# Where a LayerNorm's residual update runs in a two-layer fp32 decoder: GpSimd or VectorE

## The chip, the cores and the metric

The kernel runs on one core of one Trainium2 chip. The metric is the device time of one execution in microseconds; it is given as the median of the executions shown, with the lowest and the highest.

## What is computed

A decoder trunk of two layers over 256 tokens of width 1024, all in fp32. Each layer is a mixer (sliding-window attention, a state-space layer and a pooling branch, gated and merged), a cross-attention into 256 memory tokens, and a feed-forward part, a dense SwiGLU in layer 0 and eight experts, two per token, in layer 1. Behind each of the six parts stands the same step, on the residual stream x:

```python
def layer_norm(x, g, b):
    mu = jnp.mean(xf, axis=-1, keepdims=True)
    var = jnp.mean(jnp.square(xf - mu), axis=-1, keepdims=True)
    y = (xf - mu) * lax.rsqrt(var + LN_EPS)
    return (y * g + b).astype(x.dtype)
...
    for i in range(DEPTH):
        h = hybrid_mixer(x, ...)
        x = layer_norm(DN_ALPHA * x + h, ln1_g[i], ln1_b[i])
        c = memory_cross_attention(x, mem, ...)
        x = layer_norm(DN_ALPHA * x + c, ln2_g[i], ln2_b[i])
        f = swiglu(x, ...) if i % 2 == 0 else moe_swiglu(x, ...)
        x = layer_norm(DN_ALPHA * x + f, ln3_g[i], ln3_b[i])
```

## The kernel before

**Weights.** TensorE multiplies fp32 numbers in three passes: each number is cut into a high part that the fast fp32 format holds and a low part, the rest, and the product is high x high, low x high and high x low (`mm3`, L279 to L282). The activations are cut once. The weights arrive as chunks of 1 MB, and each half of a chunk is cut when it is first asked for (`parts`): ScalarE copies the 128x1024 half into `whi` (L217), VectorE subtracts that from the raw half into `wlo` (L220). There are three `whi` and three `wlo` buffers and three raw chunks (more in the expert stage); so ScalarE and VectorE cut at most three halves ahead of TensorE, and a half's buffer comes free when its last matmul is done. Half a chunk is eight blocks of 128x128, and so 24 matmuls in the products of 128x256.

**Order of the work.** Every engine takes its own instructions in a fixed order, which a scheduler lays down when the program is built: it simulates the engines, and of the instructions that could go next takes the one of higher priority. An instruction's priority comes from its place in the program; `tc.high_priority()` lifts a whole block, and an offset shifts it. `tc.issue_after(i)` keeps an instruction behind instruction i in that order. A `Line` object (L229) does this for its calls, so that the instructions made through one `Line` are taken in the order of the calls. The profile shows everything made through a `Line` under one line, L237 (or under that of a helper, as L220).

**The LayerNorms.** `layer_norm_in` (L309 to L383) serves five of the six. Four are of kind "xt", and the text calls them by number: **N1** behind the mixer of layer 0 (some 248 to 275 us into the span), **N2** behind its cross-attention (366 to 392), **N3** behind its SwiGLU (588 to 615), **N4** behind the mixer of layer 1 (835 to 862). The fifth, of kind "moe" (from 940), and the last one, inside the expert stage, are not touched. In a LayerNorm of kind "xt", for both halves m of the tokens:

- VectorE adds ALPHA * x to the part's result out of PSUM into `lny` (two buffers `ys`), takes mean and variance (`bst`, `bmv`) and adds EPS (`bve`); GpSimd raises that to the power -0.5 (`brs`, one column); VectorE makes the shift -mean * `brs` (`bnb`, one column, function `shift`).
- ScalarE normalizes `lny` in place, two halves of 512 columns for each m; TensorE transposes it into PSUM (`pt`).
- In four steps q, ScalarE applies gain and shift to the transposed tile, into `lnx` (128x512, two buffers), and VectorE cuts `lnx`: a cast into `xhi` and a subtraction into `xlo`. The text calls these two a pair. The next matmuls of the program take `xhi` and `xlo`, pair by pair.
- Last, x itself is brought up to date, which the next LayerNorm reads, some 80 us later or more: x = lny * g + b in the natural layout, for m = 0 and 1, on rows of 1024. These four instructions run on GpSimd, whose line `gp` holds the two powers and then these. The gains `g` and `b` were loaded by two DMAs at the start.

```python
            for m in range(2):
                gp(GP.tensor_mul, x[:, m, :], ys[m], g)
                gp(GP.tensor_add, x[:, m, :], x[:, m, :], b)
```

While a LayerNorm runs, TensorE is given other work: N1 to N3 stand beside matmuls of the memory's keys (`keys`, operands `m_hi` and `m_lo`, result copied by ScalarE to `xkt`), and so does N4. The high priority of the LayerNorm puts its VectorE work ahead of the `wlo` of the weights; `guard` (L271 to L274) keeps two of the `wlo` behind the last `bnb`.

What follows behind each: N1 the queries of the cross-attention (L280 to L282); N2 the SwiGLU, with VectorE preparing the state-space layer of layer 1 (`bgh`, `tmps`) and GpSimd clearing its tables; N3 the mixer of layer 1, for which GpSimd clears `up`, `sa`, `sb` (L758 to L760) and works out 16 table instructions first (L827 to L834, in `ssm_quad`); N4 the queries again. GpSimd's queue has besides these one early DMA of x (L1021); the weights come over SP's queue.

Of the kernel before, what the change touches and what calls it, by code (L numbers as in the profile page):

```python
# [39 lines left out]
ALPHA = (2.0 * L) ** 0.25  # L40
EPS = 1e-5
NFIFO = 3
NFX = 11
MAGIC = 12582912.0
TWO_PI = 2.0 * math.pi
SIN_SCALE = 6.2831850

# columns of the per-layer parameter block
PC = {}
# [7 lines left out]

# columns of the constant block: for both layers, for the layers' attention, for the routing
CC = {}
# [136 lines left out]
def tile_trunk(ctx, tc, x_in, xt_in, memt_in, w_in, par_in, ln_in, lnt_in, wr_in, br_in, cst_in, out):  # L196
    nc = tc.nc

    V, A, T, GP = nc.vector, nc.scalar, nc.tensor, nc.gpsimd
# [27 lines left out]

    # calls whose instructions an engine takes in the order of the calls
    class Line:  # L229
# [27 lines left out]

    # the two parts of a chunk, each half of it split when it is first asked for
    def parts(raw):
# [24 lines left out]
    x = xp.tile([P, 2, D], F32, name="x")  # L284
# [6 lines left out]

    # the first loads, in the order of their use
    xt = [xp.tile([P, KD, S], F32R, tag=n, name=n) for n in ("xhi", "xlo")]
# [12 lines left out]

    # x <- LayerNorm(ALPHA * x + f); kind "xt" also gives the transposed result in two parts, kind "moe" the natural
    # one in two parts with the router's logits
    def layer_norm_in(l, i, f, end, kind, lp, r):  # L309
        g = lp.tile([P, D], F32, name="lng", bufs=1)  # L310
        b = lp.tile([P, D], F32, name="lnb", bufs=1)
# [8 lines left out]
        ys, pts = [], []  # L320
        dv, ac, te, gp = Line(), Line(), Line(end), Line()
# [51 lines left out]
        if kind == "xt":  # L373
            for m in range(2):
                gp(GP.tensor_mul, x[:, m, :], ys[m], g)
                gp(GP.tensor_add, x[:, m, :], x[:, m, :], b)
        else:
            dv(V.tensor_add, x[:, 1, :], x[:, 1, :], b)
            for m in (1, 0):
                ac(hi_of, xhi[:, m], x[:, m])  # L380
# [13 lines left out]

    # out^T blocks: stationary weights, moving activations
    def ws_gemm(nob, kt, act, sink, first=0, w=None):
# [20 lines left out]

    # natural outputs: stationary activations, moving weights; n columns of up to 512 in `accs`
    def xs_step(accs, act, w, c0, k, nw, first, last):
# [11 lines left out]

    # the last chunk, one accumulator after the other
    def xs_end(accs, act, w, k0, kn, nw, start):
# [30 lines left out]

    # exp of a small tile by range reduction and a polynomial
    def exact_exp(dst, src, t):
# [16 lines left out]

    # (sine of half an angle, cosine of that, the angle's remainder in [-pi, pi])
    def half_angle(sn, cs, rr, th, t):
# [16 lines left out]

    # in steps, for other work to go between them
    def ssm_params(sp, l, mp, par, par2, tmps, b8, b4, b2):
# [27 lines left out]
        r = t("s_r")  # L532
        rr, sn, cs = t("s_rr"), t("s_sn"), t("s_cs")
        for i, _ in enumerate(zip_longest(exact_exp(r, er, t), half_angle(sn, cs, rr, th, t))):
            if i % 7 == 6:
                yield
        # powers 4 to 1 of abar
        apr, api = t4(), t4()
# [5 lines left out]
        yield  # L544
        # f = (abar - 1) / a
        inv, num = t("s_inv"), t("s_num")
        # f abar^3, f abar^2, f abar, f
        fbr, fbi = t4(), t4()
# [33 lines left out]
        yield  # L582
        # four steps at a time: decay r^4, angle 4*rr (in turns, as a short head and a tail)
        r4 = mp.tile(sh, F32, name="r4")
# [12 lines left out]

        # products of one compact matrix with four scalars each, spread into its two diagonal blocks
        def spread(dst, mr, mi, sr, si, ts, neg):
# [17 lines left out]

        # output matrices (C, -C_im), and those times powers of abar
        cx = b4([P, 2, NT, 2, 16], F32, "cx")
        GP.memset(cx, 0.0)  # L620
        for h in range(2):
            o = slice(64 * h, 64 * h + 64)
# [3 lines left out]
        GP.memset(wx, 0.0)  # L626
        # input matrices, by the step of the four, transposed to [(step, channel), state]
        bt = [mp.tile([P, NT, P], F32, name=f"bt{c}") for c in range(2)]
# [22 lines left out]
        yield  # L651
        # the four steps among themselves: blocks (from step i, to step 3 - o) = C abar^(3-o-i) B, and the direct term
        lx = mp.tile([P, NT, 4, 32], F32, name="lx")
        GP.memset(lx, 0.0)
        dm = b2([P, NT, 32], "dm")
        o = slice(96, 128)
# [12 lines left out]
    def mixer(l, xt, sc, sp, par, xk):  # L669
        with ExitStack() as es:  # L670
# [34 lines left out]

            # input of the state-space layer: by step of four, then with the steps on the partitions
            us = wk.tile([P, 4, 4, SC], F32, tag="us", name="us", bufs=1)
# [44 lines left out]
            if l == 0:  # L752
                project()
            # pooling
            up = b4([P, 4, S + 16], F32, "up")
# [32 lines left out]

            # gates and branches; the sum of the branches grows in the tile of the first gate
            def gates(idx, gt=None):  # L790
# [87 lines left out]
            def attention():  # L878
                for n in range(2):
# [4 lines left out]
                    for a in range(2):  # L884
# [32 lines left out]
                        yield  # L917
                        # the weights transposed, over the weights
                        pt = s_sb.rearrange("p h (b t) -> p h b t", b=n + 1)
# [19 lines left out]
            def state_space():  # L939
                for q in range(4):  # L940
                    yield from ssm_quad(q)
                yg = wk.tile([P, 4, 4, SC], F32, tag="us", name="yg", bufs=1)
                hold.append(yg)
                # channels back on the partitions, the steps of four one after the other
                for j in range(4):
                    for o in range(4):
                        nc.sync.dma_start(yg[32 * j:32 * j + 32, 3 - o], ux[32 * o:32 * o + 32, j])
# [4 lines left out]

            # `main` (its steps and what they weigh), with the `count` steps of `side` spread over it
            def weave(main, side, count):
# [30 lines left out]

            # gated linear unit of the state-space branch
            h_hi = wk.tile([P, 4, S], F32R, tag="us", name="h_hi", bufs=1)
# [45 lines left out]

    # blocks of the transposed keys of the memory; the last matmul
    def keys(mt, first, last, kt_=None, w=None):
# [5 lines left out]
    def cross(l, xt, kv, mt, kt_, w):  # L1041
        with ExitStack() as es:
# [9 lines left out]
            ws_gemm(8, KD, xt, lambda ob, ps: A.copy(qt[:, ob, :], ps))  # L1052
            # weights by token, then, in their place, by memory token
            wt = wk.tile([P, 2, 4 * S], F32, name="xwt", bufs=1)
# [113 lines left out]
    def moe(l, xn_hi, xn_lo, pl, dv):  # L1168
        with ExitStack() as es:
# [11 lines left out]

            # router
            lgt = mp.tile([E, S], F32, name="lgt")
# [24 lines left out]

            # slots of the chosen tokens, from 1
            ps = pst.tile([P, 512], F32, tag="tr", name="ps")  # L1210
# [8 lines left out]

            # weights of the chosen experts, and the largest count  # L1220
            comb = t("comb")
# [27 lines left out]

            # one-hot gather of the tokens of `ne` experts, transposed, in two parts  # L1250
            def prepare(ne, slot_col, dv=None):
# [137 lines left out]
            finish_ln()  # L1389
            # tokens past the first 128 of an expert  # L1390
            n_max = nc.values_load(cnti[0:1, 0:1], min_val=0, max_val=S)
# [77 lines left out]
```

## Time and profile before

| | |
|---|---|
| time, median of 3 executions | 1968.97 us (1966.24 to 1973.69) |
| profiled execution: first to last instruction (span) | 1967.4 us |
| profiled execution: its own total time | not listed apart from the three |
| TensorE busy (PE) | 1888.8 us, 96% |
| VectorE busy (DVE) | 1549.9 us, 79% |
| ScalarE busy (ACT) | 1283.4 us, 65% |
| GpSimd busy (POOL) | 154.4 us, 8% |
| mean granted clock of TensorE | 0.980 of full speed |
| DMA | 503.37 MB, mean 256 GB/s |

The profile was taken of one execution; its times count from its first instruction. The busy share of TensorE is near 100% in the expert stage, which fills the second half of the span, and lower in the first half, where the parts depend on one another; that is where its waits are. A busy TensorE isn't always a fast one: the granted clock falls to half in some stretches. GpSimd's 8% are short bursts in a few places.

### The profile page before, as it was taken

To read this page: it belongs to the slowest core of one execution; us is meant where nothing else is said; L and a number is where in the kernel's file an instruction comes from. 1 tells how busy PE (TensorE), PEld (TensorE's weight loads), DVE (VectorE), ACT (ScalarE), POOL (GpSimd) and SP (SyncE) were. 2 spreads that over 40 slices of the span, in tenths; PEclk is the share of its full clock that TensorE was granted. 3 is DMA by queue.
4 is the path that set the end of the run, shared out by engine and by line. 5 is a ranking of instruction groups with operands and counts; after the bars stand their busy time and mean duration, and the time that the engine had idled before them with its cause. 6 is when DMAs were issued, how large, how long until landed. Compare 5 with 4: busy or idle time off the path is not lost.

```text
span 1967.4 us, 27900 instructions
## 1 busy us (share of the span) xinstructions
PE 1888.8 (96%) x10672; PEld 1639.2 (83%) x10672; DVE 1549.9 (79%) x1960; ACT 1283.4 (65%) x1673; POOL 154.4 (8%) x127
## 2 busy tenths in 40 slices
PE   7999989899998999989799999999999999999996
PEld 7998988799998998878588888888888888888875
DVE  7874774795457855664899999999999999999987
ACT  5756545466445545544588777787777878788774
POOL 4030030300006300020200000000000000000000
PEclk9999989999999999989899999999999999999998
DMA  7334544454554353585399998999989999899970
GB/s 253 129 109 139 205 164 147 145 186 154 176 196 144 140 171 118 193 331 207 111 381 372 353 374 327 369 373 354 372 327 369 374 354 372 328 368 365 380 279 23
DMA packets 74925, 503.37 MB, mean 256 GB/s; under 512 B 9505, under 2 KB 11809, under 8 KB 15265
## 3 DMA queue, kind: packets, MB, share of 16 engines
q1 hardware_dynamic: 74496, 500.43, 68.2%
q8 instruction: 85, 1.39, 0.3%
q0 software_dynamic: 144, 1.05, 0.2%
q14 instruction: 56, 0.45, 0.1%
q10 hardware_dynamic: 144, 0.05, 0.0%
HBM read 498.34 MB, written 1.05 MB: 254 GB/s over the span
## 4 chain that ended last, share of the span: by engine, by line
PE 85%; DVE 9%; ACT 3%; issue 2%; POOL 1%; DMA 0%; ACTq 0%; DVEq 0%; POOLq 0%
PE ps L280 8%; PE ps L282 8%; PE ps L281 8%; PE pu L1300 5%; PE dn L448 5%; PE pu L1301 5%; PE pg L1301 5%; PE pu L1299 5%; PE pg L1300 5%; PE dn L449 5%; PE dn L450 5%; PE pg L1299 5%; DVE wlo L220 3%; PE acc L426 2%; PE acc L428 2%
## 5 line engine op out<-in xcount | busy, mean ns | idle before, releaser
L220 DVE TENSOR_TENSOR wlo<-raw,whi 128x1024 fp32r<-128x1024 f32 x926 | 1126.1, 1237 | 317.2 <-ACT whi L217 302.4
L217 ACT ACTIVATE whi<-raw 128x1024 fp32r<-128x1024 f32 x926 | 974.3, 1060 | 512.1 <-PE ps L281 186.2
L280 PE MATMUL ps<-xhi,whi 128*128 128x256 f32 x992 | 288.4, 291 | 21.8 <-ACT whi L217 13.1
L281 PE MATMUL ps<-xlo,whi 128*128 128x256 f32 x992 | 287.1, 290 | 2.2 <-DVE xlo L220 2.2
L282 PE MATMUL ps<-xhi,wlo 128*128 128x256 f32 x992 | 286.3, 289 | 1.8 <-DVE wlo L220 1.8
L280 PEld LDWEIGHTS ps<-xhi,whi 128*128 128x128 f32 x992 | 194.7, 197 | 23.8 <-ACT whi L217 13.8
L281 PEld LDWEIGHTS ps<-xlo,whi 128*128 128x128 f32 x992 | 195.3, 197 | 3.5 <-DVE xlo L220 2.7
L282 PEld LDWEIGHTS ps<-xhi,wlo 128*128 128x128 f32 x992 | 194.6, 196 | 3.1 <-DVE wlo L220 2.4
L1300 PE MATMUL pu<-wlo,xg 128*128 128x512 f32 x448 | 176.1, 393 | 2.7 <-DVE wlo L220 2.7
L449 PE MATMUL dn<-wlo,hth 128*128 128x512 f32 x448 | 177.9, 400 | 0.1
L1300 PE MATMUL pg<-wlo,xg 128*128 128x512 f32 x448 | 176.4, 394 | 1.4 <-DVE wlo L220 1.4
L1301 PE MATMUL pg<-whi,xg 128*128 128x512 f32 x448 | 175.5, 392 | 0.6 <-DVE xg L1252 0.6
L1299 PE MATMUL pg<-whi,xg 128*128 128x512 f32 x448 | 175.1, 391 | 0.0
L1301 PE MATMUL pu<-whi,xg 128*128 128x512 f32 x448 | 174.8, 390 | 0.0
L1299 PE MATMUL pu<-whi,xg 128*128 128x512 f32 x448 | 174.8, 390 | 0.0
L450 PE MATMUL dn<-whi,htl 128*128 128x512 f32 x448 | 173.8, 391 | 0.0
L448 PE MATMUL dn<-whi,hth 128*128 128x512 f32 x448 | 139.3, 390 | 0.0
L1300 PEld LDWEIGHTS pu<-wlo,xg 128*128 128x128 f32 x448 | 84.0, 188 | 27.7 <-DVE wlo L220 6.6
L1300 PEld LDWEIGHTS pg<-wlo,xg 128*128 128x128 f32 x448 | 84.0, 188 | 24.1 <-DVE wlo L220 3.8
L1299 PEld LDWEIGHTS pu<-whi,xg 128*128 128x128 f32 x448 | 84.1, 188 | 18.1
L448 PEld LDWEIGHTS dn<-whi,hth 128*128 128x128 f32 x448 | 83.9, 188 | 17.9
L1299 PEld LDWEIGHTS pg<-whi,xg 128*128 128x128 f32 x448 | 84.2, 188 | 17.4
(518 smaller groups left out, 2939.6 us busy)
## 6 DMA issues: line engine op xcount, KB each, us to landing
raw<-in_w SPq DMA_DIRECT2D x462, 1024.0 KB, 4.9
lng<-in_ln SPq DMA_DIRECT2D x6, 512.0 KB, 6.6
lnb<-in_ln SPq DMA_DIRECT2D x6, 512.0 KB, 7.4
raw<-in_memt SPq DMA_DIRECT2D x2, 1024.0 KB, 4.8
raw<-in_xt SPq DMA_DIRECT2D x4, 256.0 KB, 5.6
raw<-in_w SPq DMA_DIRECT2D x2, 512.0 KB, 5.9
ux<-us SPq DMA_DIRECT2D x32, 32.0 KB, 1.9
yg<-ux SPq DMA_DIRECT2D x32, 32.0 KB, 1.9
```

The source lines that it names most:

```text
L217: return A.activation(dst, src, AF.Copy, scale=scale)
L220: return V.tensor_sub(dst, src, hi.bitcast(F32))
L280: T.matmul(ps, whi, xhi, start=first, stop=False)
L281: T.matmul(ps, whi, xlo, start=False, stop=False)
L282: return T.matmul(ps, wlo, xhi, start=False, stop=last)
L426: T.matmul(accs[m][n], ah, wh, start=first, stop=False)
L448: T.matmul(ps, ah, wh, start=first, stop=False)
L449: T.matmul(ps, ah, wl, start=False, stop=False)
L450: return T.matmul(ps, al, wh, start=False, stop=last)
L1299: T.matmul(ps, xg[0][:, k, :], wh, start=(k == 0), stop=False)
L1300: T.matmul(ps, xg[0][:, k, :], wl, start=False, stop=False)
L1301: T.matmul(ps, xg[1][:, k, :], wh, start=False, stop=(k == KD - 1))
```

## The change

The four instructions that bring x up to date go to VectorE instead of GpSimd, in the LayerNorms of kind "xt". They are no longer part of a `Line`; their priority is lowered by 400 places, which puts them behind what the program asks for up to 400 instructions later, where that is ready; and each stands behind the last instruction of the LayerNorm's VectorE line, the subtraction of the fourth pair. The kind "moe" keeps its two on GpSimd. The rest of the diff takes out comment lines and the lines shift by one or two (L220 to L221, L237 to L238).

```diff
+LATER = 400
...
         if kind == "xt":
-            for m in range(2):
-                gp(GP.tensor_mul, x[:, m, :], ys[m], g)
-                gp(GP.tensor_add, x[:, m, :], x[:, m, :], b)
+            with tc.high_priority(offset=-LATER), tc.issue_after(dv.prev.ins):
+                for m in range(2):
+                    V.tensor_mul(x[:, m, :], ys[m], g)
+                    V.tensor_add(x[:, m, :], x[:, m, :], b)
```

Where the scheduler then puts them can be read from the order of each engine's instructions. VectorE in N1, before, from the three low parts behind the second `bnb` on (`wlo` is a weight's low part, CAST and `xlo` the pairs):

```order
L220 TENSOR_TENSOR wlo<-raw,whi 128x1024 x3
L237 CAST xhi<-lnx 128x512
L220 TENSOR_TENSOR xlo<-lnx,xhi 128x512
L237 CAST xhi<-lnx 128x512
L220 TENSOR_TENSOR xlo<-lnx,xhi 128x512
L220 TENSOR_TENSOR wlo<-raw,whi 128x1024
L237 CAST xhi<-lnx 128x512
L220 TENSOR_TENSOR xlo<-lnx,xhi 128x512
L237 CAST xhi<-lnx 128x512
L220 TENSOR_TENSOR xlo<-lnx,xhi 128x512
L220 TENSOR_TENSOR wlo<-raw,whi 128x1024 x14
```

The same place with the change, from the fourth low part on:

```order
L221 TENSOR_TENSOR wlo<-raw,whi 128x1024
L238 CAST xhi<-lnx 128x512
L221 TENSOR_TENSOR xlo<-lnx,xhi 128x512
L238 CAST xhi<-lnx 128x512
L221 TENSOR_TENSOR xlo<-lnx,xhi 128x512
L377 TENSOR_TENSOR x<-lny,lng 128x1024 x2
L221 TENSOR_TENSOR wlo<-raw,whi 128x1024
L378 TENSOR_TENSOR x<-x,lnb 128x1024
L221 TENSOR_TENSOR wlo<-raw,whi 128x1024
L378 TENSOR_TENSOR x<-x,lnb 128x1024
L221 TENSOR_TENSOR wlo<-raw,whi 128x1024 x12
```

Nothing ahead of the fourth pair moved; behind it two multiplications come ahead of the next low part, and the two additions are spread behind it. In N2 and N3 it is the same with the two multiplications; there the additions stand together behind two low parts (N2) and one (N3).

VectorE in N4, before, from the low part behind the second `bnb` to the first maximum of the cross-attention (`xmx`, `xnm`):

```order
L220 TENSOR_TENSOR wlo<-raw,whi 128x1024
L237 CAST xhi<-lnx 128x512
L220 TENSOR_TENSOR xlo<-lnx,xhi 128x512
L237 CAST xhi<-lnx 128x512
L220 TENSOR_TENSOR xlo<-lnx,xhi 128x512
L237 CAST xhi<-lnx 128x512
L220 TENSOR_TENSOR xlo<-lnx,xhi 128x512
L237 CAST xhi<-lnx 128x512
L220 TENSOR_TENSOR xlo<-lnx,xhi 128x512
L220 TENSOR_TENSOR wlo<-raw,whi 128x1024 x11
L1067 TENSOR_REDUCE xmx<-ps 128x2
L1069 TENSOR_SCALAR xnm<-xmx 128x2
```

and with the change:

```order
L238 CAST xhi<-lnx 128x512
L221 TENSOR_TENSOR xlo<-lnx,xhi 128x512
L377 TENSOR_TENSOR x<-lny,lng 128x1024 x2
L378 TENSOR_TENSOR x<-x,lnb 128x1024 x2
L221 TENSOR_TENSOR wlo<-raw,whi 128x1024 x11
L1069 TENSOR_REDUCE xmx<-ps 128x2
L1071 TENSOR_SCALAR xnm<-xmx 128x2
```

Here all four instructions stand ahead of the eleven low parts that follow the pairs.

GpSimd in N3, before, from the two powers (`brs`) to the first tables of the state-space layer:

```order
L237 TENSOR_TENSOR brs<-bve,mhalf 128x1 x2
L237 TENSOR_TENSOR x<-lny,lng 128x1024
L237 TENSOR_TENSOR x<-x,lnb 128x1024
L237 TENSOR_TENSOR x<-lny,lng 128x1024
L237 TENSOR_TENSOR x<-x,lnb 128x1024
L758 MEMSET up 128x4x16
L759 MEMSET sa 128x4x16
L760 MEMSET sb 128x3x16
L827 TENSOR_TENSOR stab<-cst,thi 128x256
L834 TENSOR_TENSOR dec<-cst,r_4416 128x256
```

and with the change:

```order
L238 TENSOR_TENSOR brs<-bve,mhalf 128x1 x2
L760 MEMSET up 128x4x16
L761 MEMSET sa 128x4x16
L762 MEMSET sb 128x3x16
L829 TENSOR_TENSOR stab<-cst,thi 128x256
L836 TENSOR_TENSOR dec<-cst,r_4416 128x256
```

GpSimd has nothing of the LayerNorm left behind the powers there, and the clearing and the tables follow them directly. On TensorE the change only shifts some neighbours; at N2 two matmuls of the next weight half come ahead of the first one with a low part that waits behind the multiplications.

## Rows read from the trace of the kernel before

**Rows 1.** Windows: stretch, length, busy us (instructions) per engine, clock, DMA share, GB/s.

```profile
272.00:278.00 6.00, 5.62 (x26) 5.62 (x27) 4.66 (x7) 3.46 (x6) 0.00 (x0) 0.50 0.25 59
279.00:285.00 6.00, 6.00 (x52) 6.00 (x52) 2.13 (x3) 2.64 (x4) 0.00 (x0) 1.00 0.57 221
...
400.00:420.00 20.00, 20.00 (x150) 19.13 (x149) 19.90 (x101) 10.43 (x15) 0.00 (x0) 1.00 0.59 204
1040.00:1080.00 40.00, 40.00 (x184) 32.90 (x183) 37.28 (x35) 31.84 (x34) 0.00 (x0) 1.00 0.99 376
```

The engines in these rows are, from the left, PE, PEld, DVE, ACT and POOL.

**Rows 2.** TensorE's waits in N1, N2, N3, N4: us in total, times, longest.

```profile
PE ps L282 <- DVE wlo L220: 3.5, 1, 3.5
PE pt L237 <- ACT lny L237: 2.3, 1, 2.3
...
PE ps L280 <- ACT xkt L1038: 5.9, 2, 5.1
...
PE ps L280 <- DVE xhi L237: 3.4, 2, 2.0
PE ps L281 <- DVE xlo L220: 2.2, 1, 2.2
...
PE ps L280 <- ACT whi L217: 5.8, 1, 5.8
PE pt L237 <- ACT lny L237: 3.1, 1, 3.1
```

**Rows 3.** Timeline of N1, VectorE, then GpSimd: start, duration, instruction, idle before.

```profile
251.86 0.16 DVE L237 SCALAR_TENSOR_TENSOR bnb<-bmv,brs 128x1 f32<-128x1 f32 x1
...
255.04 2.30 DVE L237 SCALAR_TENSOR_TENSOR bnb<-bmv,brs 128x1 f32<-128x1 f32 x1 [0.67 <-POOL brs L237]
257.26 7.86 DVE L220 TENSOR_TENSOR wlo<-raw,whi 128x1024 fp32r<-128x1024 f32 x3
...
254.97 2.35 POOL L237 TENSOR_TENSOR x<-lny,lng 128x1024 f32<-128x1024 f32 x1
```

**Rows 4.** Timeline of N2: VectorE, then TensorE behind the pairs.

```profile
373.24 5.68 DVE L220 TENSOR_TENSOR wlo<-raw,whi 128x1024 fp32r<-128x1024 f32 x3
378.85 2.62 DVE L237 CAST xhi<-lnx 128x512 fp32r<-128x512 f32 x1
381.50 2.77 DVE L220 TENSOR_TENSOR xlo<-lnx,xhi 128x512 fp32r<-128x512 f32 x1
...
392.01 4.15 DVE L513 TENSOR_SCALAR bgh<-par 128x24 f32<-128x24 f32 x1
...
389.90 0.58 PE L280 MATMUL ps<-xhi,whi 128*128 128x256 f32 x1 [5.12 <-ACT xkt L1038]
...
391.01 0.58 PE L282 MATMUL ps<-xhi,wlo 128*128 128x256 f32 x1 [0.32 <-DVE wlo L220]
```

**Rows 5.** Timeline of N4: VectorE's and TensorE's first low part behind the pairs.

```profile
856.29 3.49 DVE L220 TENSOR_TENSOR wlo<-raw,whi 128x1024 fp32r<-128x1024 f32 x3
...
857.73 0.41 PE L282 MATMUL ps<-xhi,wlo 128*128 128x256 f32 x1
```

**Rows 6.** Tile lnx, all LayerNorms: ns min/median/max, first and last start.

```profile
L237 DVE CAST xhi<-lnx x16: 419/830/4360, 265.0 to 855.2; 128x512 fp32r<-128x512 f32 x16
L220 DVE TENSOR_TENSOR xlo<-lnx,xhi x16: 691/694/2772, 269.4 to 855.7; 128x512 fp32r<-128x512 f32 x16
```

**Rows 7.** Lines by form, GpSimd: busy us, mean ns, idle before.

```profile
L237 POOL TENSOR_TENSOR x<-x,lnb 128x1024 f32<-128x1024 f32 x9 | 27.7, 3076 | 0.7
```

**Rows 8.** Timeline of N1, TensorE.

```profile
258.24 1.12 PE L237 MATMUL pt<-cst,lny 128*128 128x128 f32 x4 [2.34 <-ACT lny L237]
...
272.38 0.58 PE L282 MATMUL ps<-m_hi,wlo 128*128 128x256 f32 x1 [3.54 <-DVE wlo L220]
```

**Rows 9.** Timeline of N3: first low part after the update; first matmul using one.

```profile
616.57 1.55 DVE L220 TENSOR_TENSOR wlo<-raw,whi 128x1024 fp32r<-128x1024 f32 x1 [2.44 <-ACT whi L217]
...
615.87 0.40 PE L282 MATMUL ps<-xhi,wlo 128*128 128x256 f32 x2
```

## The prediction

> **What bounds the kernel now.** I read the waits of TensorE first, then the engines in those stretches in order of time, last the stretches behind them. The expert stage has TensorE busy all 40.00 of 40.00 us [rows 1], and VectorE there works in step with it; a microsecond won ahead of it therefore moves the whole stage forward, and with it the end. Ahead of it the long waits of TensorE that this change can touch stand behind the four LayerNorms, called N1 to N4 as above: 3.5 + 2.3, 5.1 of the 5.9, 3.4 + 2.2 and 5.8 + 3.1, together 25.4 us [rows 2]. A wait costs more than itself: from 272 to 278 TensorE is granted half its clock (1.2 instead of 2.4 GHz) and passes 26 matmuls, where the same kind passes 52 in 6 us at the full one [rows 1].
>
> Who is late? Several rows name ScalarE, but the reader should look one step behind, at VectorE beside GpSimd. In N1 the one-column step bnb takes 2.30 us where its sister took 0.16, and ends at 257.34, as GpSimd's multiplication does (254.97 + 2.35 = 257.32) [rows 3]. Three low parts take 7.86 there and 5.68 in N2, undisturbed 3.49 [rows 3 to 5]. A cast of 0.42 takes up to 4.36, a subtraction of 0.69 up to 2.77 [rows 6]. These casts free the two lnx buffers that ScalarE fills, and so ScalarE's rows are late. GpSimd's additions are 3.08 us each [rows 7].
>
> **The change, part by part.** *Removed:* sixteen GpSimd instructions, four in each of N1 to N4, some 3 us each. GpSimd's own time is worth nothing, as nobody waits for x until the next LayerNorm; what goes is what they did to VectorE. No transfer and no semaphore of a queue moves with them. *Added:* sixteen VectorE instructions of the shape of a low part, 3.49 / 3 = 1.16 us [rows 5], 4.7 per LayerNorm. They stand behind the four pairs of cast and subtraction, but ahead of some low parts: two multiplications ahead of the next one in N1 to N3, all four in N4 (the listings above). Behind them in line is the low part, and TensorE waits for that.
>
> *N1.* TensorE stopped at 255.9 (258.24 less 2.34) [rows 8]. With bnb at 0.16 ScalarE starts the second half 2.0 earlier and TensorE resumes at 256.2, after 0.3 instead of 2.3. The three low parts are done at 258.7 and all four pairs by 264.5, taking ScalarE's steps as they are and pairs at 0.42 + 0.69; the fourth low part, placed between the pairs, is done at 262.1. TensorE has 68 matmuls and 8 transposes up to it, 9.0 us at 0.115 to 0.12 each, and asks for it at 265.2: no wait, against 272.38 [rows 8]. That is 7.2; the half clock that followed (5.9 us, half of it lost, 52 against 26 [rows 1]) adds 2.6. The updates: two multiplications end at 266.8, the next low part at 268.0, asked for at 268.4. It just fits. **9.8 us.**
>
> *N2.* Here bnb was not held. Low parts at 3.5 instead of 5.68 [rows 4] and free pairs bring the last subtraction to 382.3, so TensorE, through with the keys at 384.8 (389.90 less 5.12), goes on. Two multiplications end at 384.7 and the low part at 385.8. The new order also puts two matmuls of the next weight half ahead of it, whose high part ScalarE can split only when the keys are done; so TensorE stands for 1.0 and uses the low part at 386.1 instead of 391.01 [rows 4]: 4.9, and 0.2 for the two matmuls done already. The half clock after the old wait is worth 1.5 (an estimate: some 16 matmuls, at 0.21 instead of 0.115). **6.6 us.**
>
> *N3.* GpSimd comes to its 16 table instructions of the state-space layer earlier, right behind the LayerNorm's two powers; they run beside the pairs and updates. What that costs is read behind the old updates: a low part of 1.16 took 1.55 there [rows 9], 0.4 more. TensorE's 2.0, 2.2 and 1.4 us waits for pairs go, but the pairs end near 606 (an estimate: bnb not held there, and four pairs of 0.42 + 0.69 behind ScalarE's steps), two multiplications and the low part near 610.6, used at 615.87 before [rows 9]: 5.3. TensorE has then waited about 3 us anew, and a wait of that length was followed by half clock; 2.3 of the 5.3 is lost again. **3.0 us**, bounds 0 and 5.3.
>
> *N4.* bnb, one cast and one subtraction were held by 2.1 each, as in [rows 3, 6]; without it the last pair ends at 850.1, 6.2 before 856.29 [rows 5]. But all four updates come next: 850.1 + 4.7 + 1.2 = 856.0 for the first low part, used at 857.73 before [rows 5]. 1.8, less 0.4 of half clock that lasts to the same time. **1.4 us**, bounds -1 and 2.2.
>
> Sum 9.8 + 6.6 + 3.0 + 1.4 = 20.8. The profiled span of 1967.4 becomes 1946.6. The profiled execution's own total is not given; the median 1968.97 lies 1.6 above its span, and I set the forecast against that median: **1948.2 us**.
>
> *A rule against it.* At N3 the row shows sharing: 1.55 instead of 1.16. The Trainium skill, SBUF — State Buffer, section "Who interferes with whom", states that VectorE and GpSimd share a pair of ports under an exclusive lock, and that a VectorE instruction with two SBUF inputs waits out the whole of a GpSimd instruction that reads SBUF. By that rule each of about ten VectorE instructions at N3 would stand a whole table step, N3 would gain nothing, and the sum would be 17.8, or 1951.2 us; rival 1 has N3 at nothing too. The rule agrees with bnb's 2.30 in N1; at N3 I keep to the row.
>
> **The rivals.** *1. VectorE gives part of it back.* Behind N2 VectorE is busy 19.90 of 20 us [rows 1], and bgh stood 4.15 us there under GpSimd's memsets [rows 4], which the change leaves. VectorE's blocked time between 373 and 390 is 2.2 in the three low parts, 2.2 in each of two casts and 2.1 in a subtraction [rows 4 to 6], 8.6 or so; 4.7 of updates leave 3.9, the most that N2 can win if VectorE sets the pace until 434. With N3 at 0 the sum is 9.8 + 3.9 + 1.4 = 15.1: 1953.9. For it: the full engine. Against: TensorE lost nothing in those 20 us. The Trainium skill, Perfetto Trace Analysis, section "Optimizing Scalar/DVE Operations", says that with VectorE saturated, moving work off it may make sense, even to GpSimd, and warns of the shared port; this change goes the other way, and the first half of that advice is this rival.
>
> *2. ScalarE keeps the waits.* If the two lnx buffers and the order of ScalarE's line set the pairs' pace, only bnb's delays go, 2.1 in N1 and N4, and perhaps 3 of the wait in N1: 7 us, 1962. For it: ScalarE is named in four of seven [rows 2]. Against: the casts of 4.36.
>
> *3. Slower: the updates hold the low parts.* If VectorE is not ahead of TensorE when the pairs end, each group of 4.7 lands on TensorE in full, 18.7 in four places: 1987.7 if nothing is won in return. It decides where VectorE's lead at the last pair is under two multiplications, 2.3 us; N1 has 0.4 left after them, N4 none. Against: VectorE loses more to GpSimd now, some 6 to 10 us in each of the four, than the updates cost.
>
> *4. The change doesn't do what it says:* the updates would be taken ahead of the pairs despite the low priority. The listings show them behind, so this has next to no chance.
>
> **How the numbers follow.** Forecast 0.63 (1948.2), rival 1 0.20 (1953.9), rival 2 0.10 (1962), rival 3 0.05 (1987.7), rival 4 0.02. Low ends: N1 at its bare waits 5.8, N2 3.9, N3 0, N4 -1, sum 8.7, so 1960.3; high ends 10 + 6.6 + 5.3 + 2.2 = 24.1, so 1944.9. With the runs' own scatter (1966.24 to 1973.69) the range 1942 to 1960 holds the forecast and rival 1 and leaves most of the rest out. A run of this kernel can tell about 0.5%, 9.8 us, from no change. Faster by more than that: 0.61 of the forecast's chance, 0.19 of rival 1, 0.03 of rival 2: 0.83. Within it: 0.12. Slower: 0.05.
>
> **What would show it.** No cast above about 1 us and no subtraction above 1.2 in the first, second and fourth LayerNorm; bnb at 0.16; the update's sixteen instructions on VectorE at 1.2 us each. TensorE's wait for the low part in N1 gone, that behind N2 down to about 1, a wait of about 3 for the low part in N3 and of 4 to 5 in N4. Wrong it would be if waits of 2 us and more for low parts stood behind N1 or N2, or if TensorE began to wait between 396 and 434.

## The result and the profile after

The changed kernel takes 1943.34 us (median of 4 executions, 1941.12 to 1947.30) against 1968.97 before: 0.9872 of the time, 95% interval 0.9854 to 0.9890. (A ratio here compares the executions of both kernels and can differ from the quotient of the two medians by about 0.001.) The forecast was 1948.2 with a range of 1942 to 1960, and faster. The same kernel measured once more later gave 1945.43 and 0.9884 (0.9862 to 0.9906). The profiled execution's span fell from 1967.4 to 1945.4 us, by 22.0; the sum of the prediction was 20.8. That execution was the slowest of the four, 1947.30.

| | before | after |
|---|---|---|
| span of the profiled execution | 1967.4 | 1945.4 |
| TensorE (PE) busy | 1888.8, 96% | 1882.1, 97% |
| VectorE (DVE) busy | 1549.9, 79% | 1532.6, 79% |
| GpSimd (POOL) busy | 154.4 | 110.9 |
| mean clock | 0.980 | 0.984 |

VectorE has sixteen instructions more and is busy 17.3 us less. That is the result in one line: what it did itself cost less than what it had stood beside GpSimd.

**Where the time went.** The first instruction of each LayerNorm (`lny<-x,acc`) is a good milestone, since the work between two of them is the same in both kernels. The windows view cut at these milestones, first of before, then of after (stretch, length and busy us of the engines PE, PEld, DVE, ACT and POOL, clock, DMA share, GB/s):

```profile
248.00:366.17 118.17, 112.29 (x673) 101.70 (x673) 67.83 (x77) 54.90 (x88) 15.09 (x7) 0.96 0.43 150
366.17:587.90 221.73, 215.17 (x1530) 201.52 (x1529) 147.98 (x263) 115.82 (x167) 20.31 (x10) 0.98 0.49 173
587.90:835.12 247.22, 234.47 (x1704) 219.82 (x1703) 163.49 (x253) 132.50 (x231) 48.14 (x45) 0.97 0.44 154
835.12:937.64 102.52, 93.56 (x526) 83.53 (x526) 56.12 (x70) 47.29 (x76) 11.93 (x6) 0.95 0.68 264
937.64:1967.40 1029.76, 999.72 (x4526) 812.97 (x4524) 939.83 (x941) 783.76 (x852) 14.18 (x8) 0.99 0.87 331
```

```profile
248.57:356.74 108.17, 107.96 (x673) 97.72 (x673) 61.91 (x82) 54.55 (x88) 2.88 (x3) 1.00 0.45 163
356.74:571.82 215.08, 213.17 (x1530) 199.99 (x1529) 141.03 (x267) 115.70 (x167) 9.15 (x6) 1.00 0.50 178
571.82:815.60 243.78, 234.37 (x1704) 220.45 (x1703) 160.79 (x257) 132.72 (x231) 39.45 (x41) 0.96 0.45 156
815.60:916.28 100.68, 92.60 (x525) 82.33 (x525) 53.88 (x75) 47.20 (x76) 1.12 (x2) 0.95 0.68 269
916.28:1945.40 1029.12, 999.43 (x4526) 813.31 (x4524) 940.03 (x941) 783.84 (x852) 14.18 (x8) 0.99 0.87 331
```

From the second column, with the terms of the prediction:

| stage | before | after | gain | predicted |
|---|---|---|---|---|
| N1 to N2 | 118.17 | 108.17 | 10.0 | 9.8 |
| N2 to N3 | 221.73 | 215.08 | 6.65 | 6.6 |
| N3 to N4 | 247.22 | 243.78 | 3.4 | 3.0 |
| N4 to the fifth | 102.52 | 100.68 | 1.8 | 1.4 |
| fifth to the end | 1029.76 | 1029.12 | 0.6 | 0 |
| start to N1 | 248.00 | 248.57 | -0.6 | 0 |

In N1 and N2 the clock is 1.00 where it was 0.96 and 0.98: with the waits, the half clock has gone. In N3 and N4 it is what it was.

**TensorE's waits**, in the stretches of N1, N2, N3 and N4 that answer to [rows 2] (us in total, times, longest):

```profile
PE pt L238 <- ACT lny L238: 0.2, 1, 0.2
...
PE ps L281 <- ACT xkt L1040: 0.8, 1, 0.8
PE ps L281 <- ACT whi L218: 0.8, 1, 0.8
...
PE ps L283 <- DVE wlo L221: 2.3, 1, 2.3
...
PE ps L281 <- ACT whi L218: 6.4, 2, 6.3
PE ps L283 <- DVE wlo L221: 0.7, 1, 0.7
```

N1 has none left worth the name. N2 has 0.8 us for `whi`, and 0.8 for `xkt` that stood there before as well (the 5.9 in two of [rows 2] less the 5.1). N3 has lost its waits for pairs and has a new one, for a low part. N4 keeps its long wait for a high part.

**VectorE in N1**, from the second `bnb` on, the timeline that answers to [rows 3], and the tile `lnx` over all LayerNorms, which answers to [rows 6]:

```profile
255.61 0.16 DVE L238 SCALAR_TENSOR_TENSOR bnb<-bmv,brs 128x1 f32<-128x1 f32 x1 [0.67 <-POOL brs L238]
255.68 3.49 DVE L221 TENSOR_TENSOR wlo<-raw,whi 128x1024 fp32r<-128x1024 f32 x3
259.09 0.42 DVE L238 CAST xhi<-lnx 128x512 fp32r<-128x512 f32 x1
...
264.72 2.35 DVE L377 TENSOR_TENSOR x<-lny,lng 128x1024 f32<-128x1024 f32 x2
266.99 1.22 DVE L221 TENSOR_TENSOR wlo<-raw,whi 128x1024 fp32r<-128x1024 f32 x1
```

```profile
L238 DVE CAST xhi<-lnx x16: 419/426/831, 259.1 to 829.3; 128x512 fp32r<-128x512 f32 x16
L221 DVE TENSOR_TENSOR xlo<-lnx,xhi x16: 691/693/987, 259.5 to 829.7; 128x512 fp32r<-128x512 f32 x16
```

bnb takes 0.16 instead of 2.30, three low parts 3.49 instead of 7.86. The longest cast is 0.83 instead of 4.36, the longest subtraction 0.99 instead of 2.77. The two multiplications end at 267.0 and the next low part is there at 268.2; the prediction had 266.8 and 268.0, counted from a milestone 0.6 us earlier.

### The profile page after: what moved, and what is told of

Same layout as the page of the kernel before. It is cut to its first block, busy times and chain, and to the rows that moved or that the text cites. A ratio compares the mean times of both kernels' runs of the same rounds, so it can differ in the third digit from the quotient of the medians.

```text
span 1945.4 us, 27894 instructions
## 1 busy us (share of the span) xinstructions
PE 1882.1 (97%) x10672; PEld 1634.6 (84%) x10672; DVE 1532.6 (79%) x1976; ACT 1283.2 (66%) x1673; POOL 110.9 (6%) x111
## 4 chain that ended last, share of the span: by engine, by line
PE 87%; DVE 8%; ACT 3%; issue 2%; DMA 0%; POOL 0%; ACTq 0%; DVEq 0%; POOLq 0%
PE ps L281 8%; PE ps L283 8%; PE ps L282 8%; PE pu L1302 5%; PE dn L450 5%; PE pu L1303 5%; PE pu L1301 5%; PE pg L1303 5%; PE pg L1302 5%; PE dn L451 5%; PE dn L452 5%; PE pg L1301 5%; DVE wlo L221 3%; PE acc L428 2%; PE acc L430 2%; PE acc L432 2%
## 5 line engine op out<-in xcount | busy, mean ns | idle before, releaser
L221 DVE TENSOR_TENSOR wlo<-raw,whi 128x1024 fp32r<-128x1024 f32 x926 | 1118.3, 1229 | 308.4 <-ACT whi L218 295.3
```

The lines of the kernel that those rows point to most:

```text
L221: return V.tensor_sub(dst, src, hi.bitcast(F32))
```

## The experiments

The theory was the prediction's: a GpSimd instruction holds VectorE's, VectorE then holds ScalarE and TensorE, and that is all the change removes; the updates themselves are paid for on VectorE, where they stand ahead of a low part. Against it stood two others: that the new place in VectorE's order is what helps, and that in N3 and N4 something else sets the end (GpSimd's tables, a load). The runs show ratios to the kernel before, each beside runs of it on the same chip; lengths of stages are taken from their profiles at the same milestones:

| kernel | ratio, 95% interval | N1 | N2 | N3 | N4 |
|---|---|---|---|---|---|
| before | 1 | 118.2 | 221.7 | 247.2 | 102.5 |
| the change | 0.9872 (0.9854 to 0.9890) | 108.2 | 215.1 | 243.8 | 100.7 |
| the change again | 0.9884 (0.9862 to 0.9906) | 108.2 | 215.1 | 238.2 | 100.9 |
| GpSimd, behind the pairs | 0.9930 (0.9914 to 0.9945) | 108.5 | 218.3 | 243.7 | 101.8 |
| no update | 0.9849 (0.9830 to 0.9869) | 108.2 | 214.0 | 238.0 | 99.3 |
| high priority | 0.9872 (0.9853 to 0.9891) | 108.2 | 214.0 | 239.7 | 100.8 |
| N4, earlier load | 0.9892 (0.9876 to 0.9908) | 108.2 | 215.1 | 238.1 | 101.6 |
| GpSimd's old work kept | 1.0072 (1.0048 to 1.0096) | 118.0 | 224.2 | 248.6 | 107.7 |
| GpSimd clearing | 0.9939 (0.9921 to 0.9958) | 109.8 | 220.7 | 244.4 | 103.7 |
| spread | 0.9868 (0.9847 to 0.9890) | 108.5 | 213.9 | 237.9 | 97.6 |
| fifth too | 0.9872 (0.9851 to 0.9892) | 108.2 | 215.1 | 238.2 | 100.8 |
| spread, fifth too | 0.9837 (0.9813 to 0.9861) | 108.5 | 213.9 | 236.6 | 97.5 |

One caution about the column N3. The same kernel, the change, gave 243.8 in one profile and 238.2 in the other, with this row of the second to be set beside the third of after:

```profile
577.49:815.67 238.18, 228.74 (x1704) 214.72 (x1703) 160.81 (x257) 132.35 (x231) 39.46 (x41) 0.99 0.45 160
```

TensorE is busy 5.6 us less for the same 1704 matmuls, at a clock of 0.99 instead of 0.96: stretches of half clock that come in one execution and not in another. So a difference of 5 us in that column says nothing by itself, and the waits have to be read instead. The stretch ahead of N1, which is the same in all these kernels, varies as well: from 247.7 to 255.6 us, and in the two profiles of the change 248.6 (clock 0.98) and 254.3 (0.96). A few microseconds between two medians may therefore have nothing to do with the LayerNorms. The columns N1 and N2 repeat within 0.1.

**Is it GpSimd's work beside VectorE, or VectorE's order?** The decisive run keeps the change, with VectorE's order around the LayerNorms unaltered, and gives GpSimd its old work back, into a tile that nothing reads:

```diff
                     V.tensor_add(x[:, m, :], x[:, m, :], b)
+            spare = lp.tile([P, D], F32, name="spare", bufs=1)
+            for m in range(2):
+                gp(GP.tensor_mul, spare, ys[m], g)
+                gp(GP.tensor_add, spare, spare, b)
```

> The change as it is (the update on VectorE, its order untouched), and GpSimd also does the old sixteen instructions in their old place, into a spare tile that nothing reads. Theory (what the change takes away is that GpSimd's two-input instructions hold VectorE's): bnb, the casts and the subtractions are held again as before, the stages behind N1 and N2 last about as long as before or longer (118 and 222 us between the starts of the LayerNorms instead of 108 and 215), and with the updates on VectorE besides the time is 0.998 to 1.006 of the kernel before. Rival (the gain comes from the order on VectorE, or from GpSimd's queue being free for its tables): N1 and N2, where nothing waits for GpSimd's queue, stay at 108 and 215, time under 0.992.

Measured 1.0072, 1981.68 us: a little above the expected range, and the whole gain is gone. Its timeline of VectorE in N1 reads like [rows 3] again:

```profile
257.68 2.30 DVE L238 SCALAR_TENSOR_TENSOR bnb<-bmv,brs 128x1 f32<-128x1 f32 x1 [0.67 <-POOL brs L238]
259.90 7.90 DVE L221 TENSOR_TENSOR wlo<-raw,whi 128x1024 fp32r<-128x1024 f32 x3
267.73 4.35 DVE L238 CAST xhi<-lnx 128x512 fp32r<-128x512 f32 x1
```

2.30, 7.90 and 4.35 against 2.30, 7.86 and 4.36 before. N1 lasts 118.0 us and N2 224.2, with 108.2 and 215.1 without that work. That shows the cause in N1 and N2: nothing there waits for what GpSimd does behind the two powers, and the order on VectorE was the change's. What is above 1.000 is put down to having both, the largest part of it in N4 (107.7 against 102.5); 2.7 us of the 10.9 by which the profile is longer than that of before lie ahead of N1.

**Which of VectorE's instructions are held?** The second run puts something else in the same place: GpSimd clears a tile, about as long as the old update, and reads next to nothing (one column ahead of each three clearings, so that they start when the update would).

```diff
                     V.tensor_add(x[:, m, :], x[:, m, :], b)
+            spare = lp.tile([P, 2 * D], F32, name="spare", bufs=1)
+            for m in range(2):
+                gp(GP.tensor_scalar, spare[:, m:m + 1], ys[m][:, 0:1], 0.0, None, op0=ALU.mult)
+                for _ in range(3):
+                    gp(GP.memset, spare, 0.0)
```

> The change as it is, and in the old place of the update GpSimd clears a spare tile six times in each of N1 to N4 (128x2048, 1.81 us each by the row of such a clearing, 11 us in all, about as long as the old update), so it writes and reads nothing. Theory (which of VectorE's instructions is held goes by what both do: behind N2 the one-input bgh and tmps ended as GpSimd's clearing did, while low parts beside it took their 1.2): casts are held up to 1.8 us each, subtractions and low parts are not; 0 to 3 us per LayerNorm, 0.988 to 0.993 of the kernel before. Rival 1 (a GpSimd instruction holds everything on VectorE): subtractions of 2 us and more, 0.997 or above. Rival 2 (an instruction that reads nothing holds nothing): casts at 0.42, time of the change, 0.987.

Measured 0.9939, a little more than the theory's 0.993 and below the first rival's 0.997. N2 lasts 5.65 us longer than with the change, where the theory allowed 3. The tile `lnx` of this kernel (ns min/median/max), then one pair of N1 and the clearings beside it:

```profile
L238 DVE CAST xhi<-lnx x16: 441/1382/1823, 258.2 to 838.7; 128x512 fp32r<-128x512 f32 x16
L221 DVE TENSOR_TENSOR xlo<-lnx,xhi x16: 691/693/983, 259.0 to 840.1; 128x512 fp32r<-128x512 f32 x16
```

```profile
259.61 1.38 DVE L238 CAST xhi<-lnx 128x512 fp32r<-128x512 f32 x1
261.03 0.69 DVE L221 TENSOR_TENSOR xlo<-lnx,xhi 128x512 fp32r<-128x512 f32 x1
...
255.01 5.71 POOL L238 MEMSET spare<- 128x2048 f32 x3
```

The casts are held, up to the length of one clearing (1.81 in the row that the expectation names), and the subtractions beside the same clearings are not: their median is 0.693, as in the change. The same holds for three low parts beside them, 3.49. So what an instruction loses goes by what both engines do, and not by GpSimd being busy. The Trainium skill, SBUF — State Buffer, section "Who interferes with whom", says that a VectorE instruction with two SBUF inputs contends with a GpSimd instruction that reads SBUF and not with one that only writes it, while a VectorE instruction in a two-port fast mode, which copies and casts can enter, contends with GpSimd. The casts' 1.82 and the subtractions' 0.693 agree with it; the mode itself isn't shown by any run.

**Is GpSimd's work cheap where low parts, and not pairs, stand beside it?** Here the update goes back to GpSimd, but behind the last pair, by a real dependence on it:

```diff
-            with tc.high_priority(offset=-LATER), tc.issue_after(dv.prev.ins):
+            with tc.high_priority(offset=-LATER):
+                gp(GP.tensor_scalar, mark, xlo[:, KD - 1, S - 1:S].bitcast(F32), 0.0, None, op0=ALU.add)
                 for m in range(2):
-                    V.tensor_mul(x[:, m, :], ys[m], g)
-                    V.tensor_add(x[:, m, :], x[:, m, :], b)
+                    gp(GP.tensor_mul, x[:, m, :], ys[m], g)
+                    gp(GP.tensor_add, x[:, m, :], x[:, m, :], b)
```

> The update is back on GpSimd, but its four instructions may start only when the fourth pair of cast and subtraction is done (a one-column GpSimd instruction ahead of them reads the end of xlo). VectorE has none of the sixteen instructions. Theory (what counts is which VectorE work GpSimd stands beside: a pair held makes ScalarE and TensorE wait, a low part that takes 2.3 to 2.7 instead of 1.16 still keeps up with a TensorE that takes 2.9 per half chunk): pairs free as with the change, low parts behind them slow, 15 to 22 us under the kernel before, so 0.987 to 0.992 of its time. Rival (GpSimd costs VectorE as much wherever it stands, and TensorE pays): under 10 us of gain, 0.995 or more.

Measured 0.9930, 0.9914 to 0.9945: between the two, with the theory's upper end, 0.992, inside the interval and the rival's 0.995 outside it. By the medians the gain is 16.2 us, just inside the theory's 15 to 22. The stages tell in part why it is between. Five low parts of N1, from its timeline of VectorE, and one of TensorE's waits in N2 (us in total, times, longest):

```profile
266.50 14.06 DVE L221 TENSOR_TENSOR wlo<-raw,whi 128x1024 fp32r<-128x1024 f32 x5 [0.67 <-ACT whi L218]
```

```profile
PE ps L283 <- DVE wlo L221: 2.8, 1, 2.8
```

In N1 a low part takes 2.81 and TensorE uses one up in about 2.9 (24 matmuls at 0.12): N1 is as short as with the change, 108.5. In N2 TensorE is near the first of them when it comes; it waits 2.8, and N2 is 3.2 us longer than with the change. So holding low parts was free in N1, where VectorE has a lead, as the theory had it, and not in N2. In N3 and N4 TensorE waits 1.1 and 1.0 for low parts, where it waits 2.3 and 0.7 with the change, so these tell neither way. N2 and N4 account for some 4 of the 7.5 to 9.6 us by which this median lies above those of the change; where the rest comes from isn't shown.

**What do the updates cost on VectorE?** Here the update of x in N1 to N4 is left out altogether:

```diff
         if kind == "xt":
-            with tc.high_priority(offset=-LATER), tc.issue_after(dv.prev.ins):
-                for m in range(2):
-                    V.tensor_mul(x[:, m, :], ys[m], g)
-                    V.tensor_add(x[:, m, :], x[:, m, :], b)
+            pass
```

> The residual update of the four LayerNorms is left out, on either engine; the x that the next LayerNorm reads is the old one. It prices the sixteen VectorE instructions. Theory (they are hidden in N1, and delay the first low part in N2, N3 and N4): TensorE's 2.3 us wait in N3 goes with its half clock, 0.9 goes in N4 and about 1 in N2; the stages behind N1 as with the change within 0.5; in all 3 to 6 us less than with the change, about 0.984 to 0.986 of the kernel before. Rival (all of it is hidden in idle time of VectorE): within 1 us of the change.

Measured 0.9849, 1938.39 us, 5 to 7 us under the two measurements of the change, though the intervals of the ratios overlap. N1 stays at 108.2, N2 is 1.1 shorter, N4 1.4 to 1.6, and TensorE's wait of 2.3 for a low part in N3 is gone; these make some 5 us. So VectorE's sixteen instructions, 18.7 us by the prediction, cost about 5 to 7.

**Does the low priority keep them off the path?**

```diff
-            with tc.high_priority(offset=-LATER), tc.issue_after(dv.prev.ins):
-                for m in range(2):
-                    V.tensor_mul(x[:, m, :], ys[m], g)
-                    V.tensor_add(x[:, m, :], x[:, m, :], b)
+            for m in range(2):
+                dv(V.tensor_mul, x[:, m, :], ys[m], g)
+                dv(V.tensor_add, x[:, m, :], x[:, m, :], b)
```

> The update on VectorE as in the change, but without the lowered priority: its four instructions are made through the LayerNorm's VectorE line at its high priority. The scheduler then puts one multiplication ahead of the first low part in N1 to N3 instead of two, and all four in N4 as in the change. Theory (an instruction of 1.16 ahead of a low part that TensorE waits for costs that much): N3 1 to 2 us less than with the change, N1, N2 and N4 within 1, in all 0 to 3 us less. Rival (the low priority keeps the updates off the path): 4 to 8 us more than with the change.

Measured 0.9872, as the change. N2 is 1.1 us shorter (214.0) and the wait of 2.3 for a low part in N3 has become two of 2.2 together. So N3's wait shrank by 0.1, not by the 1 to 2 us of the theory. The rival's 4 to 8 us did not come: the low priority is worth nothing here that the runs can tell. A likely reason, which no run tests, is that the scheduler gives a free engine what is ready, and at that moment nothing else was.

**What ends last in N4?** There the change's profile shows a wait that the prediction had not named. VectorE's low part, the load of weights on SP's queue behind it, ScalarE's high part and TensorE, from the timelines of the change:

```profile
822.70 1.22 DVE L221 TENSOR_TENSOR wlo<-raw,whi 128x1024 fp32r<-128x1024 f32 x1
...
823.94 1.28 SPq L256 DMA_DIRECT2D raw<-in_w  x3
...
832.57 2.01 ACT L218 ACTIVATE whi<-raw 128x1024 fp32r<-128x1024 f32 x2 [3.35 <-DMA raw<-in_w]
...
833.68 0.58 PE L281 MATMUL ps<-xhi,whi 128*128 128x256 f32 x1 [6.29 <-ACT whi L218]
...
836.14 0.58 PE L283 MATMUL ps<-xhi,wlo 128*128 128x256 f32 x1 [0.72 <-DVE wlo L221]
```

The low part behind the second bnb reads the last raw chunk; the load leaves as it ends (823.92 and 823.94), ScalarE, waiting for it, starts 8.6 us later, and TensorE has stood 6.3. The next run lets that low part go ahead of the statistics, by leaving out the guard for N4:

```diff
-        guard[:] = [dv.prev, 2]
+        guard[:] = [dv.prev, 0 if (l, i) == (1, 0) else 2]
```

> The change, and in N4 alone the low part that stood behind the second bnb may go earlier: it then stands among the statistics, some 3 us sooner, and with it the load of weights that waits for its raw chunk. Theory 1 (in N4 two chains end together, the load for the next high part and the updates ahead of the first low part): TensorE's 6.3 us wait for the high part shrinks to 2.5 to 4, and a wait of 3 to 5 for the low part takes its place; N4 within 1 us of the change. Theory 2 (the load alone sets the end): N4 3 us or more shorter than with the change.

TensorE's waits in its N4:

```profile
PE ps L281 <- ACT whi L218: 4.6, 1, 4.6
PE ps L283 <- DVE wlo L221: 4.2, 1, 4.2
```

The wait for the high part shrinks to 4.6 and one of 4.2 for the low part stands behind it; N4 lasts 101.6 instead of 100.7 to 100.9. That is theory 1 and not theory 2, though 4.6 is above its 2.5 to 4: with the load earlier, the updates end last. The run changes more than the load, though: the low part, now among the statistics, pushes the last subtraction back, from 14.7 to 16.1 us behind the milestone, and some of the 4.2 comes from that. The earlier load alone gives nothing; leaving out the updates alone, in the run above, gave 1.4 to 1.6, and there the 6.4 for the high part stayed.

**Taking away both, and spreading the updates.** This kernel has N1 and N2 as in the run at high priority, one of N3's four instructions behind each of four low parts, and N4's update on GpSimd behind the last pair with the guard left out:

```diff
+        if kind == "xt" and (l, i) == (1, 0):
...
+                    gp(GP.tensor_mul, x[:, m, :], ys[m], g)
+                    gp(GP.tensor_add, x[:, m, :], x[:, m, :], b)
+        elif kind == "xt" and i == 2:
+            todo = [(f_, m) for f_ in (0, 1) for m in (0, 1)]
+            for behind, (add, m) in zip(hook(), todo):
+                with tc.high_priority(offset=-LATER), tc.issue_after(dv.prev.ins), tc.issue_after(behind.ins):
...
```

`hook` asks for the next halves of the weights one after the other and hands out their low parts.

> Built from what the runs so far show: N1 and N2 with the update on VectorE at high priority; N3 on VectorE with one of the four instructions behind each of four low parts of the next stage; N4 on GpSimd behind the last pair, with the low part that holds the load let go earlier. Theory (each of N3 and N4 keeps a wait of 2 to 6 us only because updates stand ahead of low parts or the load starts late): N2 1 us, N3 1 to 3.5 us, N4 1 to 4 us less than with the change, 3 to 8 in all, 0.983 to 0.9855 of the kernel before. Rival (GpSimd's tables beside N3 and the load in N4 set the end whatever the updates do): within 2 us of the change, 0.986 or above.

Measured 0.9868, which by itself meets the rival's 0.986 or above; the interval (0.9847 to 0.9890) holds both cases. N4 is 97.6, 3 us shorter than with the change, and N2 213.9; the waits for low parts in N3 and N4 are 0.5 and none. So the time alone can't tell the two apart.

**The fifth LayerNorm**, which the change leaves, has the same fault: its second bnb takes 2.29 us in the change's profile, too, and the low parts behind it 5.64:

```profile
923.50 2.29 DVE L238 SCALAR_TENSOR_TENSOR bnb<-bmv,brs 128x1 f32<-128x1 f32 x1 [0.75 <-POOL brs L238]
925.72 5.64 DVE L221 TENSOR_TENSOR wlo<-raw,whi 128x1024 fp32r<-128x1024 f32 x3
```

```diff
-            gp(GP.tensor_mul, x[:, 0, :], ys[0], g)
-            gp(GP.tensor_add, x[:, 0, :], x[:, 0, :], b)
+            dv(V.tensor_mul, x[:, 0, :], ys[0], g)
+            dv(V.tensor_add, x[:, 0, :], x[:, 0, :], b)
```

> The change, and in the fifth LayerNorm, which the change leaves as it was, the multiplication and addition of the first half of x move from GpSimd to VectorE too. In the profile of the change its second bnb still takes 2.3 us, held by GpSimd's multiplication, and three low parts 5.6 instead of 3.5. Theory: bnb at 0.16, the low parts at 3.5, two instructions more of 1.16 ahead of the router's lnx; the path to the first experts 2 us shorter (from the fifth LayerNorm's first instruction to the end 1027 instead of 1029), too little for the median to show surely, 0.985 to 0.987. Rival (VectorE is the bound there): 1029 or more.

The same place in this run:

```profile
923.70 0.16 DVE L238 SCALAR_TENSOR_TENSOR bnb<-bmv,brs 128x1 f32<-128x1 f32 x1 [0.75 <-POOL brs L238]
...
924.92 3.49 DVE L221 TENSOR_TENSOR wlo<-raw,whi 128x1024 fp32r<-128x1024 f32 x3
```

bnb is at 0.16 and the low parts at 3.49, and from the fifth LayerNorm to the end it takes 1027.4 us, against 1028.7 and 1029.1 with the change: 1.3 to 1.7 us where 2 were expected. By its median, 0.9872, it can't be told from the change.

**Both together**, beside the change on the same chip:

> The kernel of the spread updates with the fifth LayerNorm's two instructions on VectorE besides. If the gains that the profiles show add up (3 to 4 us of waits in N2, N3 and N4, 2 in the fifth), 5 to 6 us under the change run beside it: ratio to the kernel before 0.983 to 0.985. If they don't, within 2 us of the change.

> The change itself once more, on the same chip as the two kernels beside it, for the comparison: 0.987, 1942 to 1946 us.

Measured 1935.88 us, 0.9837, and 1945.43, 0.9884, for the change. All five executions of the first (1930.96 to 1940.98) lie under all four of the second (1944.19 to 1946.95). The medians are 9.6 us apart where 5 to 6 were expected. Behind the start of N1 the two profiles differ by 7.4 us (N2 1.2, N3 1.6, N4 3.4, the fifth to the end 1.7, less 0.4 in N1), so the gains add up; another 4.0 lie ahead of N1, where the two do the same work. Its N4 is 97.5, and from the fifth LayerNorm to the end it takes 1027.0.

## Why the prediction was right, and where it was not

- **The cause** was right, and is shown by the run that gives GpSimd its old work back: in N1 the same instructions are held by the same amounts again, and N1 and N2 are long again.
- **N1 and N2** came out within 0.2 us of their terms (10.0 for 9.8, 6.65 for 6.6). The steps hold one by one: bnb at 0.16, the pairs free, the second multiplication done 18.4 us behind the milestone where 18.8 was worked out, no wait of TensorE for a low part in N1 or N2, and 0.8 for `whi` in N2 where 1.0 stood. One step of the sum for N1 doesn't come out of its own figures: half of a half clock of 5.9 us is 2.95, where 2.6 was added; with it the term would be 10.1.
- **N3**: 3.4 for 3.0, but a profile can't confirm that term so closely, since half clock elsewhere in the stage moved its length by 5.6 between two executions, so that its closeness may be luck. What can be read is the wait: 2.3 for the low part, where about 3 was named. Beside GpSimd's tables a cast took 0.81 instead of 0.42, a subtraction 0.99 instead of 0.69 and a low part 1.75 instead of 1.16:

```profile
586.96 0.81 DVE L238 CAST xhi<-lnx 128x512 fp32r<-128x512 f32 x1 [1.68 <-ACT lnx L238]
587.81 0.99 DVE L221 TENSOR_TENSOR xlo<-lnx,xhi 128x512 fp32r<-128x512 f32 x1
...
593.16 1.75 DVE L221 TENSOR_TENSOR wlo<-raw,whi 128x1024 fp32r<-128x1024 f32 x1
```

  The seven instructions up to that low part lost 0.2 to 0.6 each (the two multiplications took 2.75 instead of 2.35); the prediction had 0.4 from one row. The case in which N3 would gain nothing, weighed as the rule against the change, did not come: its waits for pairs, 5.6 us, became one of 2.3.
- **N4**: the term was nearly right (1.8 for 1.4), and so were its steps on VectorE: the last pair ends 14.7 us behind the milestone (15.0 was worked out), and the first low part, which is what ends last, is there at 20.5 (20.9). But the sign "TensorE waits 4 to 5 for the low part" failed. It waits 6.3 for the high part, whose load is late, and 0.7 for the low part. In the kernel before, the wait of 5.8 for `whi` [rows 2] was indeed ScalarE held by VectorE: these rows show ScalarE idle for VectorE's subtractions, and not for a load ahead of the high part:

```profile
850.98 1.02 ACT L237 ACTIVATE lnx<-pt,lnt 128x256 f32<-128x256 f32 x2 [3.00 <-DVE xlo L220]
...
854.17 1.02 ACT L237 ACTIVATE lnx<-pt,lnt 128x256 f32<-128x256 f32 x2 [1.91 <-DVE xlo L220]
855.08 3.19 ACT L217 ACTIVATE whi<-raw 128x1024 fp32r<-128x1024 f32 x3
```

  What I missed is the load that comes next when that hold is gone, and the sentence that no transfer moves was wrong here: the load leaves as the low part behind bnb ends, 10.5 us behind the milestone before and 8.3 with the change. That the number came out is partly luck: the two chains end 0.7 us apart, and had the load come later by more than that, it would have ended last.
- **Rival 1** (VectorE as the bound behind N2): from 387 to 425 TensorE waits nowhere, busy 38.00 of 38.00 us, though VectorE is busy 36.27 (the row below, of the windows view). It fell. **Rival 2** (ScalarE keeps the waits) fell in N1 and N2, where ScalarE's steps run as they are and TensorE waits at most 0.8 at a time for them. **Rival 3** (updates on the path) exists, at some 5 to 7 us of its 18.7, as the run without them shows. **Rival 4** did not come.

```profile
387.00:425.00 38.00, 38.00 (x276) 35.78 (x275) 36.27 (x130) 20.82 (x32) 0.00 (x0) 1.00 0.52 178
```

- **The rest of the difference**, 25.6 us in the medians against 22.0 in the profiles, lies within what executions of one kernel differ by: the profiled execution of the change, at 1947.30, is 4.0 above its median, and the change measured again gave 1945.43.

What stays open: how GpSimd's tables in N3 and VectorE share, instruction by instruction, and what N3 would take without tables beside it. That was not tried.

## What to carry to other kernels

An engine that is 8% busy can hold one that everything waits for; look for instructions that take several times as long as their sisters of the same shape, and see which instruction of the neighbour ends when they do. When such work is moved, it pays at its new place only by what stands right behind it in the queue: the run without the updates gives the most that better placing of them can bring. And when the holder of a wait is taken away, ask what is next in line for the same place, the load behind a split above all, before naming what ends last.

## What was not expected

- Not in the prediction, though expected by the time of its run: clearing on GpSimd held VectorE's casts (up to 1.82 us instead of 0.42) and left its two-input subtractions at 0.69: the light instruction of a pair lost most.
- GpSimd pays as well: of the two equal multiplications in N1 before, the first, with a one-column instruction held behind it, took 2.35 us [rows 3], the second, beside low parts, 3.36.
- Two executions of one kernel differed by 5.6 us in TensorE's busy time for the same 1704 matmuls, through half clock in stretches without a wait of this change; ahead of N1 the same two differ by 5.7 us the other way.
